# Smaller W12 loads, earlier cells and on-chip heads in the mLSTM half of a two-layer trunk

## The chip, the cores and the metric

The kernel runs on one core of a Trainium2 chip. The metric is the device time of one execution in microseconds. Three runs of the kernel before took 1699.9 to 1701.43 us, the median is 1699.91. The engines are PE (TensorE), DVE (VectorE), ACT (ScalarE), POOL (GpSimd) and SP (SyncE, which here only issues DMAs).

## The reference

The trunk has two layers on x of 512 tokens by 2048 features, all float32. Layer 0 is latent attention with 16 heads and isn't touched. Layer 1 is an mLSTM (matrix memory) with 8 heads, q and k of 128 and v of 256 features a head, and it is what the change is about:

```python
proj = x @ w_in                 # q, k, v, o, gates, z
q, k = silu(conv(q)), silu(conv(k))
# per head, equal to one causal product over the 512 tokens:
s = (q @ k.T) * DK**-0.5 * exp(decay)        # decays from the i and f gates
h = (s @ v) / max(|sum s|, exp(-m))
h = headnorm(h) * sigmoid(o) * silu(z)
x = layernorm(alpha * x + h @ w_out)
```

## The kernel before, in words

Every product is made of three passes on PE (mm3): both operands are split into a high half of a rounded type (ACT's cast, L171) and the rest (DVE's subtraction, L172). Weights come through rings in SBUF: raw (3 slots of 128x1024, 512 KB), whi and wlo (3 each) for the split halves, e (3 slots of 128x512, 256 KB), and the larger rings t, v and h. SP issues weight loads in the order that the tile framework's scheduler gives it, and each engine runs its instructions in its own order; a load that waits for a slot holds up every load behind it in SP's queue.

Layer 1 has these stages, by the time of the profile. Values by plain products end at 816 us. From 816 to 1232 five calls of quad make the other value columns and the four pairs of output gates O and Z. quad is a product of two column blocks with seven half-size products: with weight quarters W11, W12, W21, W22 (odd or even k tiles, left or right columns) its first group forms q1 (W11) and q5 (W11+W12), its second q7 (W12+W22), q6 (W11+W12+W22) and q3 (W22), its third q2 and q4. A group has four iterations, of 24, 36 and 24 matmuls; a call has 336. In the second group (L366 to L373) an iteration loads W22 and W12 as two raws, adds them in one instruction (L368), adds W22 to the kept sums t (L370), and splits all three.

From 1232 to 1430 four pairs of heads get q and k (gemm_b). The cells, one for each head, are generators that a small scheduler (tick, finish; one at a time) puts between the matmuls: a cell loads its decays (GpSimd's queue, L850), gate rows and values, makes scores (SCORES below: four blocks of 3 matmuls), exponentials (L872) and products with the values (30 matmuls), norms (L901 to L905), then yields 11 us and turns its result by 8 transposes (L907 to L912). Heads 0 to 5 store the result to a DRAM scratch gscr (L915).

From 1430 to 1697 the last projection (out_proj) multiplies the heads' results by w_out in four column blocks. The left operand comes from g1: it finishes the head's cell, reads the result back from gscr into a raw slot (L1087, k tiles 0 to 11) or takes it from SBUF (12 to 15), and splits it. Since the last cells are not done, blocks 0 and 1 are made in two parts: k tiles 0 to 11 of both, then 12 to 15 of both. Each k tile pair is one weight load (L191). The previous layer's norm gains multiply the residual on POOL (L1100, L1101); the last norm's gains and biases are broadcast by SP's queue (L1076).

Of the kernel before, what the change touches and what calls it, by code (L numbers as in the profile page):

```python
# [66 lines left out]
class Ahead:  # L67


    def __init__(self, makers, ahead):  # L70
        self.makers, self.ahead, self.items = makers, ahead, []

    def __len__(self):
        return len(self.makers)

    def __getitem__(self, i):
        while len(self.items) < min(i + 1 + self.ahead, len(self.makers)):
            self.items.append(self.makers[len(self.items)]())
        return self.items[i]


class Kern:
# [216 lines left out]
    def quad(self, w, c0, c1, x, S, done):  # L299

        nc = self.nc
        V = nc.vector
        n = KT // 2  # L310
        a, b = self.banks
        self.banks = b, a
        two = lambda f: [f(), f()]
        half = lambda v, j: v[:, 512 * j : 512 * j + 512]

        def raw(par, i, c):

            t = self.rt()
            src = w[2 * i * P : (2 * i + 4) * P, c : c + 512].rearrange("(k q p) c -> p q k c", p=P, q=2)
            nc.sync.dma_start(t.rearrange("p (k c) -> p k c", k=2), src[:, par])  # L320
            return t

        def taken(t):
            hi, lo = self.wh(), self.wl()
            self.split(t, hi, lo)
            return hi, lo

        def taken2(t):
            hi, lo = self.wh(), self.wl()
            for j in range(2):  # L330
                self.split(t[j], half(hi, j), half(lo, j))
            return hi, lo

        def mul(ps, op, j, i, hl):

            for d in range(2):
                o = op(i + d)
                for m in range(2):
                    s = slice(j * 256 + m * P, j * 256 + (m + 1) * P)
                    self.mm3(ps[m], (o[0][:, s], o[1][:, s]), (half(hl[0], d), half(hl[1], d)),  # L340
                             i + d == 0, i + d == n - 1)
                self.tick()

        xe, xo = (lambda i: x[2 * i]), (lambda i: x[2 * i + 1])
        se, so = (lambda i: S[i][0]), (lambda i: S[i][1])
        q1, q5 = two(a), two(a)
        t = []
        for i in range(0, n, 2):
            w11 = raw(0, i, c0)
            t.append([self.t(), self.t()])  # L350
            for j in range(2):
                w12 = self.e()
                kt = 2 * (i + j)
                nc.sync.dma_start(w12, w[kt * P : (kt + 1) * P, c1 : c1 + 512])
                V.tensor_tensor(t[-1][j], half(w11, j), w12, op=ALU.add)
            mul(q1, xe, 0, i, taken(w11))
            mul(q5, so, 1, i, taken2(t[-1]))
            self.some(2)
        e1, e5 = two(self.t), two(self.t)
        for m in range(2):  # L360
            nc.scalar.copy(e1[m], q1[m])
        for m in range(2):
            nc.scalar.copy(e5[m], q5[m])

        q7, q6, q3 = two(b), two(a), two(b)
        for i in range(0, n, 2):  # L366
            w22, w12 = raw(1, i, c1), raw(0, i, c1)
            V.tensor_tensor(w12, w12, w22, op=ALU.add)  # L368
            for j in range(2):
                V.tensor_tensor(t[i // 2][j], t[i // 2][j], half(w22, j), op=ALU.add)  # L370
            mul(q7, se, 1, i, taken(w12))
            mul(q6, se, 0, i, taken2(t[i // 2]))
            mul(q3, so, 0, i, taken(w22))  # L373
        u, c12 = two(self.t), two(self.t)
        for m in range(2):
            V.tensor_tensor(u[m], q6[m], e1[m], op=ALU.add)

        def sums(m):
            V.tensor_tensor(e5[m], e5[m], u[m], op=ALU.subtract)
            V.tensor_tensor(u[m], u[m], q7[m], op=ALU.add)  # L380

        def upper(m):
            V.tensor_tensor(c12[m], e5[m], q3[m], op=ALU.add)
            done(m, 1, c12[m])

        def lower(m):
            V.tensor_tensor(e5[m], e5[m], q7[m], op=ALU.subtract)
            done(2 + m, 1, e5[m])

        self.pending += [partial(f, m) for f in (sums, upper, lower) for m in range(2)]  # L390
        q2, q4 = two(a), two(a)
        for i in range(0, n, 2):
            w21 = raw(1, i, c0)
            for j in range(2):
                V.tensor_tensor(t[i // 2][j], t[i // 2][j], half(w21, j), op=ALU.add)  # L395
            mul(q2, xo, 0, i, taken(w21))
            mul(q4, xo, 1, i, taken2(t[i // 2]))
            self.some(2)

        def left(tb, v, q):  # L400
            V.tensor_tensor(v, v, q, op=ALU.add)
            done(tb, 0, v)

        self.pending += [partial(left, c + m, v[m], q[m]) for c, v, q in ((0, e1, q2), (2, u, q4)) for m in range(2)]
# [317 lines left out]

    def out_proj(self, w_out, g, resid, finish, last=1, early=0):

        nc = self.nc  # L730
        r, tasks = {}, []
        stats = {tb: self.const.tile([P, 4, 6], F32, tag="bn", bufs=4, name=self.name("bn")) for tb in range(NTB)}

        def block(toks, cb, ks=(0, KT), last=1):
            for tb in toks if ks[0] == 0 else ():
                t = r[tb, cb] = self.h() if early and cb < 2 else self.t()
                resid(tb, cb, t)
            out = self.gemm_a(w_out, cb * 512, g, toks, last, ks)
            for tb in toks:
                t = r[tb, cb]  # L740
                nc.vector.scalar_tensor_tensor(t, t, 1.0 if ks[0] else ALPHA, out[tb], op0=ALU.mult, op1=ALU.add)
                if ks[1] == KT:
                    nc.vector.bn_stats(stats[tb][:, cb], t)

        every = (0, 1, 2, 3)
        for ks in ((0, early), (early, KT)) if early else ((0, KT),):
            for cb in range(2):
                block(every, cb, ks)
        for toks in ((0, 1), (2, 3)):
            block(toks, 2)  # L750
            block(toks, 3, last=last if toks[0] else 1)
            moments = {}
            for tb in toks:
                mv, a = self.small(2, 4), self.small()
                nc.vector.bn_aggr(mv, stats[tb])
                nc.vector.tensor_scalar(a, mv[:, 1:2], EPS, None, ALU.add)
                moments[tb] = mv[:, 0:1], self.rsqrt_small(a)
            tasks.append(self.add(finish(toks, r, moments)))
        return tasks
# [90 lines left out]
            self.nc.gpsimd.dma_start(d[sb], self.R[sb][hd : hd + 1, :].broadcast_to([P, SEQ - sb * P]))  # L850
        return d

    def cell(self, hd, q, k, vscr, ascr, out, gscr, rows):


        nc, V = self.nc, self.nc.vector
# [46 lines left out]
        for tb in range(NTB):  # L903
            t = hn[tb // 2][:, tb % 2]
            nc.scalar.activation(t, t, AF.Copy, scale=y[:, tb : tb + 1])  # L905
        yield 11.0
        for j in range(2):  # L907
            tp = self.ps()
            for tb in range(NTB):
# [42 lines left out]
    def mlstm(self, w_in, x, gscr, late):  # L952
# [32 lines left out]
        for pair in range(H1 // 2):  # L985
            q_ps = self.gemm_b(w_in, 0, pair * 256, x)
            q = [self.conv_silu(q_ps[j], 2 * pair + j) for j in range(2)]
            k_ps = self.gemm_b(w_in, 0, O_K + pair * 256, x)
            k = [self.conv_silu(k_ps[j], 8 + 2 * pair + j) for j in range(2)]
            for j in range(2):  # L990
                hd = 2 * pair + j
                out = [self.h() if hd < H1 - 1 else self.e() for _ in range(2)]
                cell = self.cell(hd, q[j], k[j], vscr, ascr, out, gscr if pair < 3 else None, rows)
                t = self.add(cell, 0.0 if j else 4.0)
                tasks.append((t, out))
        return tasks

# [2 lines left out]
def hybrid_trunk_kernel(ctx: ExitStack, tc: tile.TileContext, x, positions, mla_w_in, mla_q_norm, mla_w_qb, mla_kv_norm,  # L1000
# [70 lines left out]
    K.width = 1  # L1071
    cells = K.mlstm(ml_w_in[0], x1, gscr, Turned())

    def bcast(src, cb, home=K.h):
        t = home()
        nc.sync.dma_start(t, src[0:1, cb * 512 : (cb + 1) * 512].broadcast_to([P, 512]))  # L1076
        return t

    def g1(i):
        def f():  # L1080
            task, gate = cells[i // 2]
            K.finish(task)
            hi, lo = K.h(F32R), K.h(F32R)
            t = gate[i % 2]
            if i < 12:
                t = K.rt()[:, :SEQ]
                nc.sync.dma_start(t, gscr[i * P : (i + 1) * P])  # L1087
            K.split(t, hi, lo)
            return hi, lo

        return f
# [14 lines left out]
    def finish1(toks, r, moments):  # L1106
        for tb in toks:
            for cb in range(4):
                if cb not in ln1:
                    ln1[cb] = bcast(ln_w[1:2], cb, home), bcast(ln_b[1:2], cb, home)  # L1110
                w, b = ln1[cb]
                t = r[tb, cb]
                nc.vector.scalar_tensor_tensor(t, t, moments[tb][0], w, op0=ALU.subtract, op1=ALU.mult)
# [1 line left out]
                nc.sync.dma_start(rows(out[0], tb, cb), t)  # L1115
                yield 2.0

    for t in K.out_proj(ml_w_out[0], Ahead([g1(i) for i in range(KT)], 2), resid1, finish1, 5, 12):
        K.finish(t)


# [29 lines left out]
```

## Time and profile before

| | |
|---|---|
| median of 3 runs | 1699.91 us |
| profiled execution | 1698.93 us, its span 1697.2 |
| PE busy | 1625.4 us, 96% of the span |
| DVE, ACT, POOL busy | 65%, 44%, 9% |
| DMA | 230.06 MB, 136 GB/s mean |
| mean granted TensorE clock | 0.987 |

PE is the engine that is nearly always busy, and its time is spent in one kind of instruction, a matmul of 128x512. An idle engine other than PE costs nothing by itself. What counts are the stretches in which PE's busy time is less than the stretch, or in which its granted clock is under 1.00; a wait there is followed back from PE to the engine, the load and the slot that came last.

### The profile page before, as it was taken

Reading aid. Unit: us, or ns where it says so; the run is one execution under the profiler, and the core shown is the slowest. Engines: PE = TensorE matmul, PEld = TensorE weight load, DVE = VectorE, ACT = ScalarE, POOL = GpSimd, SP = SyncE. Lnnn points to the kernel's source line nnn. Section 1 sums busy time; section 2 is a strip of 40 time slices with the busy share of each in tenths; the row PEclk is TensorE's granted clock in tenths of the full one; section 3 lists DMA queues with packets and bytes.
Section 4 is the critical chain, followed back from the end, with each engine's and each line's share of the span. In section 5 each row is a group of like instructions: output and inputs, shape, how many; then the busy total and the mean of one; then the engine's idle time right before and its main releaser. Section 6 shows DMA issues by size and latency. Waiting matters only on the chain.

```text
span 1697.2 us, 20582 instructions
## 1 busy us (share of the span) xinstructions
PE 1625.4 (96%) x7466; PEld 1338.7 (79%) x7466; DVE 1100.6 (65%) x1904; ACT 740.7 (44%) x1192; POOL 151.7 (9%) x254
## 2 busy tenths in 40 slices
PE   8999999999999999999999998998999998779996
PEld 6888888888888888778877776876788887668875
DVE  3374222677778535888686867786786566755677
ACT  3343222554555323454434544554445555553332
POOL 1000000000000000110000000000011110423600
PEclk9999999999999999999999999999999999989998
DMA  7333333322223436678555565555546842666454
GB/s 206 106 96 100 99 95 86 99 64 56 82 63 93 149 100 190 218 222 167 165 137 161 126 147 112 164 135 121 99 126 150 145 131 86 215 188 206 158 197 163
DMA packets 174182, 230.06 MB, mean 136 GB/s; under 512 B 23592, under 2 KB 97416, under 8 KB 174080
## 3 DMA queue, kind: packets, MB, share of 16 engines
q1 hardware_dynamic: 164528, 204.11, 45.2%
q0 software_dynamic: 7248, 20.44, 3.9%
q10 hardware_dynamic: 2304, 4.20, 0.8%
q8 instruction: 58, 0.95, 0.2%
q14 instruction: 44, 0.36, 0.1%
HBM read 206.51 MB, written 19.96 MB: 133 GB/s over the span
## 4 chain that ended last, share of the span: by engine, by line
PE 70%; DMA 14%; DVE 11%; issue 2%; ACT 2%; POOL 1%; SPq 0%; DVEq 0%; POOLq 0%; ACTq 0%
PE acc L206 58%; PE ps L206 10%; DMA raw<-in_ml_w_in_dram 9%; DVE wlo L172 5%; PE ps L203 2%; DMA raw<-in_ml_w_out_dram 1%; DVE raw L368 1%; ACT whi L171 1%; DMA e<-vscr 1%; DVE t L395 1%; DMA e<-in_ml_w_in_dram 1%; POOL s L264 0%; DMA gscr<-h 0%; DVE t L370 0%; DMA raw<-in_mla_w_out_dram 0%
## 5 line engine op out<-in xcount | busy, mean ns | idle before, releaser
L206 PE MATMUL acc<-whi,h 128*128 128x512 f32 x1656 | 537.8, 398 | 15.6 <-ACT whi L171 15.2
L172 DVE TENSOR_TENSOR wlo<-raw,whi 128x1024 fp32r<-128x1024 f32 (+1 forms) x311 | 377.6, 1216 | 269.0 <-ACT whi L171 254.5
L171 ACT CAST whi<-raw 128x1024 fp32r<-128x1024 f32 (+2 forms) x315 | 324.5, 1030 | 518.0 <-PE acc L206 344.7
L206 PE MATMUL acc<-h,whi 128*128 128x512 f32 x1536 | 471.9, 392 | 0.0
L206 PEld LDWEIGHTS acc<-whi,h 128*128 128x128 f32 x1656 | 315.2, 191 | 81.5 <-ACT whi L171 16.7
L206 PE MATMUL acc<-wlo,h 128*128 128x512 f32 x828 | 329.7, 398 | 12.0 <-DVE wlo L172 11.8
L206 PEld LDWEIGHTS acc<-h,whi 128*128 128x128 f32 x1536 | 286.2, 188 | 58.2 <-issue 1.0
L206 PE MATMUL acc<-h,wlo 128*128 128x512 f32 x736 | 287.4, 390 | 0.0
L206 PEld LDWEIGHTS acc<-wlo,h 128*128 128x128 f32 x828 | 158.0, 191 | 50.3 <-DVE wlo L172 18.7
L206 PEld LDWEIGHTS acc<-h,wlo 128*128 128x128 f32 x736 | 138.5, 188 | 29.5
L206 PE MATMUL ps<-whi,h 128*128 128x512 f32 x488 | 156.5, 392 | 0.0
L206 PEld LDWEIGHTS ps<-whi,h 128*128 128x128 f32 x488 | 92.4, 189 | 19.3
L206 PE MATMUL ps<-wlo,h 128*128 128x512 f32 x244 | 97.0, 397 | 10.2 <-DVE wlo L172 10.2
L171 ACT CAST whi<-t 128x512 fp32r<-128x512 f32 x120 | 68.6, 618 | 59.0 <-PE ps L206 35.3
L206 PE MATMUL acc<-whi,v 128*128 128x512 f32 x248 | 84.7, 400 | 0.0
L172 DVE TENSOR_TENSOR wlo<-t,whi 128x512 fp32r<-128x512 f32 x120 | 77.4, 685 | 9.0 <-ACT whi L171 9.0
L206 PEld LDWEIGHTS ps<-wlo,h 128*128 128x128 f32 x244 | 46.2, 189 | 23.8 <-DVE wlo L172 14.4
L203 PE MATMUL ps<-ident,t 128*128 128x128 f32 x352 | 57.6, 280 | 7.1 <-DMA t<-in_x_dram 6.4
L206 PE MATMUL ps<-h,h 128*128 128x128 f32 (+3 forms) x288 | 60.3, 323 | 4.1 <-DVE t L878 4.1
L702 ACT ACTIVATE t<-ps,s 128x128 f32<-128x128 f32 (+3 forms) x64 | 33.7, 527 | 65.2 <-DVE s L701 65.1
L203 PEld LDWEIGHTS ps<-ident,t 128*128 128x128 f32 x352 | 45.2, 144 | 20.9 <-issue 3.7
L370 DVE TENSOR_TENSOR t<-t,raw 128x512 f32<-128x512 f32 x40 | 26.6, 688 | 49.2 <-DMA raw<-in_ml_w_in_dram 49.2
(216 smaller groups left out, 1762.9 us busy)
## 6 DMA issues: line engine op xcount, KB each, us to landing
raw<-in_ml_w_in_dram SPq DMA_DIRECT2D x136, 512.0 KB, 4.9
raw<-in_mla_w_in_dram SPq DMA_DIRECT2D x48, 512.0 KB, 3.8
raw<-in_mla_w_out_dram SPq DMA_DIRECT2D x48, 512.0 KB, 3.8
raw<-in_ml_w_out_dram SPq DMA_DIRECT2D x48, 512.0 KB, 4.1
e<-in_ml_w_in_dram SPq DMA_DIRECT2D x40, 256.0 KB, 5.1
t<-in_x_dram SPq DMA_DIRECT2D x16, 256.0 KB, 6.5
raw<-in_mla_w_kvb_dram SPq DMA_DIRECT2D x16, 256.0 KB, 3.4
raw<-in_mla_w_kvb_dram SPq DMA_DIRECT2D x32, 128.0 KB, 2.6
```

The costliest lines, as they stand in the source:

```text
L171: a = self.nc.scalar.copy(hi, src)
L172: b = self.nc.vector.tensor_tensor(lo, src, hi.bitcast(F32), op=ALU.subtract)
L203: self.nc.tensor.transpose(out, in_, ident)
L206: self.nc.tensor.matmul(out, lhsT, rhs, start=start, stop=stop)
L368: V.tensor_tensor(w12, w12, w22, op=ALU.add)
L370: V.tensor_tensor(t[i // 2][j], t[i // 2][j], half(w22, j), op=ALU.add)
L395: V.tensor_tensor(t[i // 2][j], t[i // 2][j], half(w21, j), op=ALU.add)
L702: nc.scalar.activation(pt[bi], s[:, :n], AF.Exp, bias=b, scale=scale, accum_out=tot)
```

## The change

1. In quad W12 is loaded as two e tiles of 256 KB by a new helper, right(i), in the first group as before and in the second group in place of a raw; the addition and the split there are made by halves.
2. Only heads 0 to 3 go through gscr. g1 reads back k tiles 0 to 7.
3. A cell marks its task as free before the wait ahead of its transposes, and the wait is 15 in place of 11, so that the next cell can start in that time.
4. In the last projection block 0 still has k tiles 0 to 11 first, block 1 now 0 to 13; Ahead, which makes the left operands two tiles ahead, doesn't go beyond the part's last tile.
5. The last norm's broadcasts are issued by GpSimd's queue.

```diff
@@ right(i), new in quad
+            t = two(self.e)
+            for j in range(2):
+                kt = 2 * (i + j)
+                nc.sync.dma_start(t[j], w[kt * P : (kt + 1) * P, c1 : c1 + 512])
+            return t
@@ quad, second group
-            w22, w12 = raw(1, i, c1), raw(0, i, c1)
-            V.tensor_tensor(w12, w12, w22, op=ALU.add)
+            w22, w12 = raw(1, i, c1), right(i)
+            for j in range(2):
+                V.tensor_tensor(w12[j], w12[j], half(w22, j), op=ALU.add)
...
-            mul(q7, se, 1, i, taken(w12))
+            mul(q7, se, 1, i, taken2(w12))
@@ Ahead
-        while len(self.items) < min(i + 1 + self.ahead, len(self.makers)):
+        while len(self.items) < max(i + 1, min(i + 1 + self.ahead, self.limit)):
@@ out_proj
+            g.limit = ks[1]
...
-        for ks in ((0, early), (early, KT)) if early else ((0, KT),):
-            for cb in range(2):
-                block(every, cb, ks)
+        for cb in range(2):
+            block(every, cb, (0, early[cb]))
+        for cb in range(2):
+            if early[cb] < KT:
+                block(every, cb, (early[cb], KT))
@@ cell
-        yield 11.0
+
+        me[0].free = True
+        yield 15.0
@@ mlstm
-                cell = self.cell(hd, q[j], k[j], vscr, ascr, out, gscr if pair < 3 else None, rows)
+                me = []
+                cell = self.cell(hd, q[j], k[j], vscr, ascr, out, gscr if pair < 2 else None, rows, me)
                 t = self.add(cell, 0.0 if j else 4.0)
+                me.append(t)
@@ g1
-            if i < 12:
+            if i < 8:
@@ finish1
-                    ln1[cb] = bcast(ln_w[1:2], cb, home), bcast(ln_b[1:2], cb, home)
+                    ln1[cb] = bcast(ln_w[1:2], cb, home, nc.gpsimd), bcast(ln_b[1:2], cb, home, nc.gpsimd)
@@ the call
-    for t in K.out_proj(ml_w_out[0], Ahead([g1(i) for i in range(KT)], 2), resid1, finish1, 5, 12):
+    for t in K.out_proj(ml_w_out[0], Ahead([g1(i) for i in range(KT)], 2), resid1, finish1, 5, (12, 14)):
```

How this moves the queues shows at three places. SP's queue before, at the second group of the third call of quad (raw1872 and raw1873 are W22 and W12 of the first iteration; the e tiles between are the next call's):

```order
L320 DMA raw1872_8663<-in_ml_w_in_dram 128x2x512
L354 DMA e1939_9073<-in_ml_w_in_dram 128x512
L320 DMA raw1873_8665<-in_ml_w_in_dram 128x2x512
L354 DMA e1940_9076<-in_ml_w_in_dram 128x512
L354 DMA e1948_9125<-in_ml_w_in_dram 128x512
L320 DMA raw1880_8720<-in_ml_w_in_dram 128x2x512
L320 DMA raw1881_8722<-in_ml_w_in_dram 128x2x512
L320 DMA raw1888_8777<-in_ml_w_in_dram 128x2x512
L320 DMA raw1889_8779<-in_ml_w_in_dram 128x2x512
L320 DMA raw1896_8834<-in_ml_w_in_dram 128x2x512
L320 DMA raw1897_8836<-in_ml_w_in_dram 128x2x512
```

SP's queue in the same place after the change (raw1880, 1889, 1898 and 1907 are the four W22, the e tiles the halves of W12):

```order
L320 DMA raw1880_8703<-in_ml_w_in_dram 128x2x512
L328 DMA e1881_8705<-in_ml_w_in_dram 128x512
L320 DMA raw1889_8765<-in_ml_w_in_dram 128x2x512
L328 DMA e1882_8706<-in_ml_w_in_dram 128x512
L328 DMA e1890_8767<-in_ml_w_in_dram 128x512
L320 DMA raw1898_8827<-in_ml_w_in_dram 128x2x512
L328 DMA e1891_8768<-in_ml_w_in_dram 128x512
L328 DMA e1899_8829<-in_ml_w_in_dram 128x512
L320 DMA raw1907_8889<-in_ml_w_in_dram 128x2x512
L328 DMA e1900_8830<-in_ml_w_in_dram 128x512
L328 DMA e1908_8891<-in_ml_w_in_dram 128x512
```

Eight raws have become four with eight halves (e1909, the last, is the next row). The second half of an iteration (e1882, e1891, e1900) stands behind the next iteration's W22.

SP's queue before, in the last projection ahead of k tiles 8 to 11 and into block 1 (head 5's result is stored by L915 and read back by L1087 ahead of a weight tile, L191):

```order
L863 DMA t2655_12788<-ascr_6436 128x2x256
L863 DMA t2656_12789<-ascr_6436 128x2x256
L1076 DMA v2871_13918<-in_ln_w_dram 128x512
L1076 DMA v2872_13920<-in_ln_b_dram 128x512
L915 DMA gscr_83<-h2379_11589 128x512
L915 DMA gscr_83<-h2380_11590 128x512
L1087 DMA raw2648_12765<-gscr_83 128x512
L1087 DMA raw2651_12771<-gscr_83 128x512
L191 DMA raw2663_12830<-in_ml_w_out_dram 128x2x512
L191 DMA raw2720_13058<-in_ml_w_out_dram 128x2x512
L191 DMA raw2731_13112<-in_ml_w_out_dram 128x2x512
```

The same place after, from the last head that goes through gscr (head 3) on:

```order
L928 DMA gscr_83<-h2326_11268 128x512
L928 DMA gscr_83<-h2327_11269 128x512
L1102 DMA raw2591_12526<-gscr_83 128x512
L1102 DMA raw2594_12532<-gscr_83 128x512
L191 DMA raw2604_12588<-in_ml_w_out_dram 128x2x512
L191 DMA raw2632_12718<-in_ml_w_out_dram 128x2x512
L191 DMA raw2679_12918<-in_ml_w_out_dram 128x2x512
L191 DMA raw2700_13000<-in_ml_w_out_dram 128x2x512
L191 DMA raw2705_13048<-in_ml_w_out_dram 128x2x512
L191 DMA raw2717_13106<-in_ml_w_out_dram 128x2x512
L191 DMA raw2726_13173<-in_ml_w_out_dram 128x2x512
```

After head 3 weight tiles follow one another with no store, no read back and no broadcast between them.

PE before, in the fourth pair's q projection (L203 are the transposes of head 1, acc the projection; head 2's scores come 30 rows further on):

```order
L206 MATMUL acc2382_11592<-h1338_6085,whi2384_11594 128x512
L206 MATMUL acc2382_11592<-h1337_6084,wlo2385_11595 128x512
L203 MATMUL ps2386_11623<-ident_69,t2345_11394 128x128 x2
L203 MATMUL ps2386_11623<-ident_69,t2346_11395 128x128 x2
L203 MATMUL ps2387_11629<-ident_69,t2345_11394 128x128 x2
L203 MATMUL ps2387_11629<-ident_69,t2346_11395 128x128 x2
L206 MATMUL acc2381_11591<-h1344_6105,whi2400_11669 128x512
L206 MATMUL acc2381_11591<-h1345_6106,whi2400_11669 128x512
L206 MATMUL acc2381_11591<-h1344_6105,wlo2401_11670 128x512
L206 MATMUL acc2381_11591<-h1348_6120,whi2400_11669 128x512
```

PE after, in the third pair's k projection, where head 1 is turned (ps2411 is a block of head 2's scores):

```order
L206 MATMUL acc2375_11533<-h1397_6275,whi2409_11702 128x512
L206 MATMUL acc2375_11533<-h1396_6274,wlo2410_11703 128x512
L206 MATMUL ps2411_11715<-h2269_10984,h2319_11252 128x128
L206 MATMUL ps2411_11715<-h2270_10985,h2319_11252 128x128
L206 MATMUL ps2411_11715<-h2269_10984,h2320_11253 128x128
L203 MATMUL ps2412_11722<-ident_69,t2351_11406 128x128 x2
L203 MATMUL ps2412_11722<-ident_69,t2352_11407 128x128 x2
L203 MATMUL ps2413_11728<-ident_69,t2351_11406 128x128 x2
L203 MATMUL ps2413_11728<-ident_69,t2352_11407 128x128 x2
L206 MATMUL acc2375_11533<-h1403_6295,whi2409_11702 128x512
L206 MATMUL acc2375_11533<-h1404_6296,whi2409_11702 128x512
```

Head 2's scores, which stood behind head 1's transposes, now stand ahead of them, and in the projection before.

## Rows read from the trace of the kernel before

**Rows 1.** The page's part 1: busy us, share of the span, instructions.
```profile
PE 1625.4 (96%) x7466; PEld 1338.7 (79%) x7466; DVE 1100.6 (65%) x1904; ACT 740.7 (44%) x1192; POOL 151.7 (9%) x254
```

**Rows 2.** Table of stages: window, its us, busy us by engine, PEclk, DMA share, GB/s.
```profile
816.00:1232.00 416.00, 394.05 (x1683) 315.57 (x1682) 310.25 (x418) 189.37 (x260) 14.78 (x36) 0.99 0.57 135
976.00:1065.40 89.40, 80.38 (x338) 63.73 (x338) 64.14 (x87) 39.40 (x55) 2.16 (x4) 0.98 0.64 139
1065.40:1143.80 78.40, 77.58 (x337) 62.71 (x336) 63.26 (x87) 39.44 (x55) 2.16 (x4) 1.00 0.53 139
1232.00:1430.00 198.00, 198.00 (x935) 165.94 (x934) 131.64 (x227) 105.19 (x170) 22.31 (x57) 1.00 0.56 131
1430.00:1545.00 115.00, 90.64 (x427) 73.66 (x426) 73.57 (x177) 66.37 (x145) 33.92 (x55) 0.88 0.65 200
```

**Rows 3.** PE's waits, 816 to 1232: us in total, times, longest.
```profile
PE acc L206 <- DVE wlo L172: 11.1, 11, 2.4
PE ps L206 <- DVE wlo L172: 10.7, 11, 2.4
```

**Rows 4.** DVE's waits in the same stretch.
```profile
DVE t L370 <- DMA raw<-in_ml_w_in_dram: 49.2, 18, 4.4
DVE raw L368 <- DMA raw<-in_ml_w_in_dram: 26.2, 15, 3.2
DVE t L395 <- DMA raw<-in_ml_w_in_dram: 19.5, 5, 5.0
```

**Rows 5.** Chain of waits, third call of quad: start us, us, what.
```profile
1006.67 1.24 DVE raw L368
...
1010.38 6.42 DMA raw<-in_ml_w_in_dram
1016.90 1.23 DVE raw L368
...
1043.79 21.76 PE ps L206 x96
```

**Rows 6.** DVE's groups, 816 to 1232: shapes, count, busy us, mean ns, idle before.
```profile
L172 DVE TENSOR_TENSOR wlo<-raw,whi 128x1024 fp32r<-128x1024 f32 x79 | 96.0, 1221 | 2.9 <-ACT whi L171 1.2
L172 DVE TENSOR_TENSOR wlo<-t,whi 128x512 fp32r<-128x512 f32 x120 | 77.4, 685 | 9.0 <-ACT whi L171 9.0
L370 DVE TENSOR_TENSOR t<-t,raw 128x512 f32<-128x512 f32 x40 | 26.6, 688 | 49.2 <-DMA raw<-in_ml_w_in_dram 49.2
...
L368 DVE TENSOR_TENSOR raw<-raw,raw 128x1024 f32<-128x1024 f32 x20 | 24.5, 1224 | 26.2 <-DMA raw<-in_ml_w_in_dram 26.2
```

**Rows 7.** The page's part 6: count, KB, median us to landing.
```profile
raw<-in_ml_w_in_dram SPq DMA_DIRECT2D x136, 512.0 KB, 4.9
...
e<-in_ml_w_in_dram SPq DMA_DIRECT2D x40, 256.0 KB, 5.1
```

**Rows 8.** PE's waits, 1430 to 1545.
```profile
PE acc L206 <- ACT whi L171: 15.2, 5, 5.9
PE ps L206 <- DVE t L878: 4.9, 3, 3.2
```

**Rows 9.** PE's timeline there: start, us, instruction, [idle before, releaser].
```profile
1482.77 1.20 PE L206 MATMUL acc<-whi,h 128*128 128x512 f32 x4 [2.42 <-ACT whi L171]
...
1503.69 2.08 PE L206 MATMUL acc<-whi,h 128*128 128x512 f32 x4 [5.94 <-ACT whi L171]
...
1522.56 2.07 PE L206 MATMUL acc<-whi,h 128*128 128x512 f32 x4 [3.80 <-ACT whi L171]
```

**Rows 10.** SP's timeline ahead of k tiles 8 and 9.
```profile
1495.69 2.86 SPq L1087 DMA_DIRECT2D raw<-gscr  x2
1498.65 0.39 SPq L191 DMA_DIRECT2D raw<-in_ml_w_out_dram  x1
```

**Rows 11.** ACT's timeline ahead of k tiles 4 and 5.
```profile
1464.11 0.72 ACT L872 ACTIVATE t<-t,ones 128x512 f32<-128x512 f32 x1 [1.95 <-DMA t<-decay]
1464.74 1.03 ACT L171 CAST whi<-raw 128x1024 fp32r<-128x1024 f32 x1
```

More of the change, by code (lines that the diff above doesn't have):

```diff
@@ L70, in __init__ @@
     def __init__(self, makers, ahead):
-        self.makers, self.ahead, self.items = makers, ahead, []
+        self.makers, self.ahead, self.items, self.limit = makers, ahead, [], len(makers)
     def __len__(self):
@@ L321, in raw, with right @@
             return t
+        def right(i):
+            t = two(self.e)
[3 more added lines that the diff above has]
+            return t
         def taken(t):
@@ L350, in quad @@
             t.append([self.t(), self.t()])
+            w12 = right(i)
             for j in range(2):
[L352 to L355, printed above, removed]
+                V.tensor_tensor(t[-1][j], half(w11, j), w12[j], op=ALU.add)
             mul(q1, xe, 0, i, taken(w11))
@@ L721, in attend, with out_proj @@
         nc.vector.tensor_tensor(g, o, g, op=ALU.mult)
-    def out_proj(self, w_out, g, resid, finish, last=1, early=0):
+    def out_proj(self, w_out, g, resid, finish, last=1, early=(KT, KT)):
         nc = self.nc
@@ L735, in block @@
             for tb in toks if ks[0] == 0 else ():
-                t = r[tb, cb] = self.h() if early and cb < 2 else self.t()
+                t = r[tb, cb] = self.h() if cb < 2 and early[cb] < KT else self.t()
                 resid(tb, cb, t)
+            g.limit = ks[1]
             out = self.gemm_a(w_out, cb * 512, g, toks, last, ks)
@@ L851, in decays, with cell @@
         return d
-    def cell(self, hd, q, k, vscr, ascr, out, gscr, rows):
+    def cell(self, hd, q, k, vscr, ascr, out, gscr, rows, me):
         nc, V = self.nc, self.nc.vector
@@ L1072, in hybrid_trunk_kernel, with bcast @@
     cells = K.mlstm(ml_w_in[0], x1, gscr, Turned())
-    def bcast(src, cb, home=K.h):
+    def bcast(src, cb, home=K.h, eng=nc.sync):
         t = home()
-        nc.sync.dma_start(t, src[0:1, cb * 512 : (cb + 1) * 512].broadcast_to([P, 512]))
+        eng.dma_start(t, src[0:1, cb * 512 : (cb + 1) * 512].broadcast_to([P, 512]))
         return t
```

## The prediction

> **What bounds the kernel now.** I read the page's busy shares first: PE is busy for 1625.4 of 1697.2 us [rows 1], so nothing that DVE, ACT, GpSimd or a queue does can pay except where PE waits or runs at a lower clock. The table of stages says where that is [rows 2]. The four q/k projections with their cells (1232 to 1430) have PE busy for 198.00 of 198.00 us: nothing to win there, only something to lose. Two stages lose time. The five calls of quad (816 to 1232) take 416.0 us with 394.05 us of PE. The first part of the last projection (1430 to 1545) takes 115.0 us with 90.64 us of PE, at a granted clock of 0.88.
>
> For the quads the floor comes from the chain: 96 matmuls in a row take 21.76 us, or 0.2267 us each [rows 5]; a call has 336, so 76.2 us, and five have 380.8: 35.2 us are lost. The loss is uneven: the fourth call takes 78.40 us, the third, which runs the same code, 89.40 [rows 2]. What PE waits for is the low half of a split by DVE, 22 times, 21.8 us in sum [rows 3]; what DVE waits for one step earlier is a raw weight tile from HBM: 26.2 us at L368 and 49.2 us at L370, both of the second group, 19.5 us at L395, the start of the third [rows 4]. The chain of the third call shows the cycle: a load, the addition of W12 and W22 at L368, a split, and the split's end releases the slot for which the next load waited, 6.42 us in that place [rows 5]. So it is a ring that is too short for its use: an iteration of the second group takes two 512 KB raws out of three slots, lasts 36 x 0.2267 = 8.2 us when PE runs through, and the second raw of the next iteration can't be issued before W22 of this one is split. After that split come the landing (4.9 us, [rows 7]), the addition (1.22), a cast and a subtraction (1.22, [rows 6]): 7.3 us and the cast, and the split itself ends a few us into its iteration. That doesn't fit 8.2 us whenever a load is late.
>
> In the last projection PE waits 15.2 us for ACT's cast of a weight tile (5 waits) and 4.9 us for a cell's scores [rows 8]. The three large ones come straight after a cell's 30 value products: 2.42 us (k tiles 6 and 7), 5.94 (8 and 9) and 3.80 (10 and 11) [rows 9]. The casts are late because the loads are: SP's queue first waits for a head's output to be written to DRAM, then issues the loads that read it back (1495.69, 2.86 us), and only at 1498.65 the weight tile [rows 10]. With 24.4 us of idle PE and (1 - 0.88) x 115 = 13.8 us of slower clock the stage loses 38.2 us.
>
> **The change part by part.** My sums stand against the profiled execution, 1698.9 us (span 1697.2 and 1.7 around it); the median of the runs, 1699.9, is 1.0 above it, which I add at the end.
>
> W12 in halves. Per iteration of the second group one 512 KB raw goes, two 256 KB tiles of the e ring come, 20 iterations in all. Now one raw per iteration uses three slots, so W22 of the next iterations can be under way while this one is split, and the cycle above is gone. What is late next is the e ring: three slots, two tiles an iteration, each held from issue to its addition, 5.1 us of landing [rows 7] and 0.69 of addition [rows 6], at least 2 x 5.8 / 3 = 3.9 us of an 8.2 us iteration. By order the halves of the next iteration are issued between the raws, half an iteration or more ahead. So I expect every call to run like the fourth: 5 x 78.4 = 392.0, 24.0 less than 416.0 [rows 2]. I keep 2.0 of it back for the switch from the first group to the second, where raws and halves still stand in one queue: **22 us**. Bounds: 35 if all of the loss goes (416.0 - 380.8); 10 if only the waits of whole tiles go, about half of [rows 3]; below nothing only by the rival on small loads. DVE pays: 2 x 0.688 + 2 x 0.685 = 2.75 us for 1.224 + 1.221 = 2.45 [rows 6], 0.3 us an iteration, 6 us in all; DVE is busy 64.1 of 89.4 us in the third call [rows 2], so that lies in its waits; without this cover it would cost those 6 us. ACT's two casts for one are covered likewise (39.4 of 89.4). SP issues one load more, at 0.39 us [rows 10], in a queue that mostly waits for slots.
>
> The profile speaks of halves in one more way: a 256 KB tile lands in 5.1 us, a 512 KB raw in 4.9 [rows 7], so halving the size buys no latency here, and two in flight together cost none either. The Trainium skill ("DMA: Bandwidth & Descriptors", section "Bandwidth", measured) advises batching DMAs to 1 MiB or more, and its fit (section "Anatomy of one DMA") has 2.0 us of fixed cost in each; by it, as an estimate, two halves in turn need 5.2 us where one raw needs 3.2. That speaks against this edit by 2 us an iteration, 40 in all, if the loads went one after the other and were the bound: the sum would then be 1704 and not 1664.
>
> Heads 4 and 5 stay in SBUF (6 and 7 did before). Four stores and four reads of 256 KB go, and with them SP's wait for the store and the 2.86 us of reading back ahead of a weight tile [rows 10]. The waits before k tiles 8 to 11 are 5.94 + 3.80 us [rows 9]. Of the 13.8 us of slower clock, spread over five stalls, I give them two shares, 5.5 us. That is 15.2. The wait of 2.42 us stays in some form, since head 3 still takes the way through DRAM.
>
> The next cell begins before the transposes of the last one. The same matmuls in another order; one cell more (head 3) gets its scores between projection matmuls, where PE is full, and the tail has a dense cell less. That gives some of the start of the projection back, which I put at 3 us, since 38.2 less the named waits and their clock leaves about 18 us for the start, transposes and scores, of which a sixth goes. Against it: cell 5's and 7's value products now stand closer to their scores, and POOL's queue has cell 5's decay loads between L1100's multiplications, so an exponential can wait in ACT ahead of a weight cast as at 1464.11 (1.95 us for the decays, the cast behind it) [rows 11]: 3 us. The split of column block 1 at tile 14 moves two k tiles forward; it costs no instruction, and removes the wait for head 6's tiles from the end.
>
> Norm broadcasts from GpSimd: 8 issues leave SP, at 0.4 us about 3 us of a queue that held weight loads; they now stand in POOL's queue, behind cell 5's masks and ahead of cell 6's decays, and wait for v slots there. Nothing on the path either way, -2 to +2.
>
> The tail so gives 15.2 + 3 - 3 = **15 us**, between 0 (all stalls only move) and 28. In the q/k stage I take **1 us of loss** (0 to 5): the exponentials of a cell begun earlier stand in ACT ahead of weight casts.
>
> Sum: 1698.9 - 22 - 15 + 1 = 1662.9, and with the 1.0 to the median **1664 us**.
>
> **The rivals.** *Small loads are the new bound.* The e ring, not the raw ring, closes the cycle: for it speak the 5.1 us of landing and that an e load waits in SP's queue behind raws; against it 3.9 us of 8.2. Then the quads keep their 416 and only the tail moves: 1699.9 - 15 + 1 = 1686. Chance 0.12.
>
> *The tail's stalls only move.* PE stands in order, and after each cell's value products it again waits for the next weight cast, because the cell's own casts and exponentials fill ACT, not because of DRAM. For it: the waits are for ACT by name [rows 8]; against it: at 1498.65 the load itself was issued late [rows 10]. Only the quads gain: 1699.9 - 22 = 1678. Chance 0.18.
>
> *Nothing comes of it.* The raws were late through the DMA engines and not the ring (their landing of 4.9 us is a median; the share of the queues is 0.64 in the third call against 0.53 in the fourth [rows 2]), and the tail's stalls move: 1697 to 1703. Chance 0.06.
>
> *Slower.* In the stage that loses nothing today each cell is begun while the last one's work still waits; its decays aren't there, ACT stops in order at the exponential, and the weight cast behind it is late, as in [rows 11]. If each of eight cells costs a wait as long as the longest of this kind, 5.94 us [rows 9], that is 47.5 us against 36 gained: 1664 + 47.5 = 1711. It decides against the change from 4.5 us a cell on. Against it: no wait of PE in that stage now. Chance 0.05.
>
> *More than I count.* All of the quads' loss and the upper end of the tail: 1699.9 - 35 - 28 = 1637, or between that and 1646. Chance 0.03.
>
> **How the numbers follow.** The forecast's case has 0.56. Its own range is 1650 to 1676, from the bounds 10 to 35 and 0 to 28, not all at an end at once. The second rival (1678) and most of the first (1686, so to 1688) have to be inside for 8 in 10; nothing, slower and the far end stay outside: 1646 to 1688. A measurement of this kernel can't tell changes within 0.2%, 3.4 us, from none. Faster by more than that: the forecast, the first two rivals and the last, 0.89; same: 0.06, the third; slower: 0.05, the fourth.
>
> **What would show it.** Right: DVE's waits at L368 and L370 for raws fall from 75 us to under 20; the third and fifth call take 78 to 81 us; SP's queue has no store and read back for heads 4 and 5; the waits for a weight cast at k tiles 8 to 11 are under 2 us; the clock of the first part of the last projection is above 0.92. Wrong: DVE waits for e tiles in the second group (first rival); as many us of PE idle in the tail, with ACT's exponentials ahead of the casts (second); PE idle in the q/k stage (fourth).

## The result and the profile after

The changed kernel takes 1677.55 us (median of 4 runs, 1674.63 to 1680.66) where the kernel before takes 1700.67 beside it; the ratio is 0.9863, with a 95% interval of 0.984 to 0.9885. That is 23 us less; forecast were 36 (1664 us), and the range was 1646 to 1688. The profiled execution has a span of 1677.4 us.

The table of stages after (window, its us, busy us of PE, PEld, DVE, ACT, POOL, then PEclk, DMA share, GB/s) stands against [rows 2]: all five calls of quad, then the third, fourth and fifth, the q/k stage, and the start of the last projection.

```profile
816.60:1217.80 401.20, 390.56 (x1681) 316.29 (x1680) 312.36 (x458) 192.87 (x280) 14.73 (x36) 0.99 0.58 140
972.80:1057.70 84.90, 79.44 (x337) 63.76 (x336) 64.22 (x95) 40.14 (x59) 2.16 (x4) 0.98 0.67 146
1057.70:1134.40 76.70, 76.70 (x338) 63.09 (x338) 64.46 (x95) 39.90 (x59) 2.16 (x4) 1.00 0.56 145
1134.40:1217.80 83.40, 79.64 (x337) 63.83 (x336) 59.80 (x89) 39.78 (x59) 5.26 (x18) 0.98 0.58 114
1217.80:1425.20 207.40, 207.40 (x997) 174.58 (x996) 141.29 (x266) 121.51 (x205) 28.21 (x70) 1.00 0.56 138
1425.20:1503.20 78.00, 58.90 (x264) 48.13 (x264) 49.54 (x104) 42.40 (x87) 26.90 (x37) 0.85 0.62 186
```

The quads take 401.2 us, 14.8 less than 416.0. The fourth call is now near its floor (76.7 us, where 336 matmuls of 0.2267 make 76.2), but the third still takes 84.9 and the fifth 83.4. All that follows the quads took 1697.2 - 1232.0 = 465.2 us before and takes 1677.4 - 1217.8 = 459.6: 5.6 less. The q/k stage still has PE busy throughout.

PE's waits in the quads fell from 21.8 us [rows 3] to 10.6. DVE's waits after, against [rows 4]:

```profile
DVE t L402 <- DMA raw<-in_ml_w_in_dram: 38.0, 10, 5.3
DVE e L375 <- DMA e<-in_ml_w_in_dram: 21.7, 15, 4.6
DVE wlo L172 <- ACT whi L171: 18.8, 16, 7.9
DVE t L377 <- DMA raw<-in_ml_w_in_dram: 9.6, 7, 3.2
```

L375 and L377 are what L368 and L370 were: 31.3 us in place of 75.4. L402 (W21 added to the kept sum, L395 before) waits twice as long as it did (19.5 us [rows 4]).

In the last projection PE's waits after, from 1425 to 1504 (none of these four comes again later), against [rows 8]:

```profile
PE ps L206 <- ACT h L925: 7.2, 1, 7.2
PE acc L206 <- ACT whi L171: 4.5, 2, 3.9
PE ps L206 <- DVE t L889: 3.0, 1, 3.0
PE ps L206 <- DVE t L910: 1.9, 1, 1.9
```

The casts of weight tiles cost 4.5 us and not 15.2, and none of that lies ahead of k tiles 8 to 11, where [rows 9] had 9.74 (5.94 and 3.80). But there is a new wait of 7.2 us, for ACT's copy of a turned head (L925). The chain of waits behind it (start us, us, what):

```profile
1480.11 0.84 POOL v L1091 x2
1480.95 0.22 issue
1481.16 13.06 DMA t<-decay
1494.23 0.02 issue
1494.25 0.72 ACT t L883
1494.97 0.58 ACT h L925
1495.55 0.04 issue
1495.60 1.33 PE ps L206 x5
```

The head of it is one of the moved broadcasts (L1091), on GpSimd. POOL's timeline there (idle before and its releaser in brackets):

```profile
1479.51 0.60 POOL L1091 DMA_DIRECT2D v<-in_ln_w_dram  x1 [22.10 <-PE ps L206]
1480.11 0.54 POOL L1091 DMA_DIRECT2D v<-in_ln_b_dram  x1
1480.64 0.54 POOL L1091 DMA_DIRECT2D v<-in_ln_w_dram  x1
1481.16 1.06 POOL L861 DMA_DIRECT2D t<-decay  x2
```

GpSimd's queue stands for 22.1 us at a broadcast whose v slot is still in use, and head 6's decay loads (L861) are the next after the three broadcasts. They land 13.06 us after their issue, behind the broadcasts in the same queue, where the median of these loads is 4.6. ACT's exponential (L883) waits for them, and the copy that PE needs is behind the exponential:

```profile
1494.25 0.72 ACT L883 ACTIVATE t<-t,ones 128x512 f32<-128x512 f32 x1 [7.69 <-DMA t<-decay]
1494.88 1.25 ACT L925 ACTIVATE h<-ps,par 128x512 f32<-128x512 f32 x2
```

Two things come together here. ACT is free for the exponential at 1486.56 (1494.25 less 7.69), so decays issued at 1481.16 that landed in the median 4.6 us would still have been in time: the 22.1 us of standing used up all the slack that they had. Then they landed 8.5 us later than the median, while the DMA engines were busy for 95% of 1481.2 to 1494.2, at 258 GB/s. How much of that is the broadcasts ahead of them in the queue and how much SP's loads of that stretch isn't separated.

So the theory to test: the quad edit and the edits of the cells work, each for less than forecast; the moved broadcasts give some 7 us back; and what is left in quads three and five is loads. Ratios below are to the kernel before, measured beside each; intervals are 95%.

### The profile page after: what moved, and what is told of

It reads as the page before. It is cut to its first block, busy times and chain, and to the rows that moved or that the text cites. A ratio compares the mean times of both kernels' runs of the same rounds, so it can differ in the third digit from the quotient of the medians.

```text
span 1677.4 us, 20661 instructions
## 1 busy us (share of the span) xinstructions
PE 1619.5 (97%) x7466; PEld 1338.1 (80%) x7466; DVE 1108.0 (66%) x1944; ACT 748.6 (45%) x1216; POOL 158.1 (9%) x262
## 4 chain that ended last, share of the span: by engine, by line
PE 70%; DMA 12%; DVE 11%; issue 3%; ACT 2%; POOL 1%; SPq 0%; DVEq 0%; POOLq 0%; ACTq 0%
PE acc L206 56%; PE ps L206 12%; DVE wlo L172 4%; DMA raw<-in_ml_w_in_dram 4%; DMA e<-in_ml_w_in_dram 3%; PE ps L203 2%; DMA t<-decay 1%; ACT whi L171 1%; DMA raw<-in_ml_w_out_dram 1%; DMA e<-vscr 1%; DVE t L402 1%; DVE e L375 1%; POOL s L264 1%; DVE t L377 0%; DVE bn L752 0%
## 5 line engine op out<-in xcount | busy, mean ns | idle before, releaser
L172 DVE TENSOR_TENSOR wlo<-raw,whi 128x1024 fp32r<-128x1024 f32 (+1 forms) x291 | 357.7, 1232 | 260.9 <-ACT whi L171 251.1
L171 ACT CAST whi<-raw 128x1024 fp32r<-128x1024 f32 (+2 forms) x295 | 303.4, 1029 | 436.0 <-PE acc L206 323.7
L203 PE MATMUL ps<-ident,t 128*128 128x128 f32 x352 | 58.1, 282 | 9.7 <-DMA t<-in_x_dram 6.4
L203 PEld LDWEIGHTS ps<-ident,t 128*128 128x128 f32 x352 | 44.8, 144 | 23.7 <-ACT t L916 4.8
L206 PEld LDWEIGHTS ps<-h,h 128*128 128x128 f32 x288 | 48.5, 191 | 13.3 <-ACT h L925 7.5
```

Of the source, the lines that this page charges most:

```text
L171: a = self.nc.scalar.copy(hi, src)
L172: b = self.nc.vector.tensor_tensor(lo, src, hi.bitcast(F32), op=ALU.subtract)
L203: self.nc.tensor.transpose(out, in_, ident)
L206: self.nc.tensor.matmul(out, lhsT, rhs, start=start, stop=stop)
```

## The experiments

**The quad edit alone.** The kernel before with right(i) in both groups, as in the change.

> The kernel before with the edit of quad alone (W12 in 256 KB halves in both groups). In the changed kernel the five calls took 401.2 us from first matmul to the next stage's first, against 416.0 before. Theory: the raw ring's cycle is gone and nothing outside quad depends on it, so 1700.7 - 14.8 = 1686 us (1683 to 1689). Rival, as the prediction had it: 22 us from this edit, so 1679, with the rest of the gain in the changed kernel eaten by a loss elsewhere in it that the sum of stages hides.

Measured: 1682.24 us, ratio 0.9898 (0.9881 to 0.9914), 17 us less. The calls take 400.8 us in its trace, as in the changed kernel. The median lies 0.8 us below the theory's range, and by the interval (1679.5 to 1685.2 us) the rival's 1679 is only just out. A trace is one execution: in the five traces of kernels without this edit the calls take 415.9 to 419.2 us, in the five with it and no other edit of quad's code 399.0 to 402.9, and the means are 17 us apart, as the runs say. That it is the slots of the raw ring that count, and not the size or the order of the loads, rests on the waits (DVE's for raws at the two additions fell from 75.4 to 8.6 us in this trace, 7.0 and 1.6); no run gives the ring a fourth slot and keeps the whole loads.

**All but the quad edit.**

```diff
-            w22, w12 = raw(1, i, c1), right(i)
-            for j in range(2):
-                V.tensor_tensor(w12[j], w12[j], half(w22, j), op=ALU.add)
+            w22, w12 = raw(1, i, c1), raw(0, i, c1)
+            V.tensor_tensor(w12, w12, w22, op=ALU.add)
```

> The changed kernel with the edit of quad undone (one raw for W12 in the second group); all else as changed. Theory: the tail's edits are worth 5 to 8 us by themselves, so 1692 to 1696 us. Rival: the tail's edits are worth the predicted 14 and the profiled execution shows less by chance: 1687.

Measured: 1690.31 us, 0.9943 (0.9929 to 0.9957): 9.7 us by the ratio, between the two expectations. The calls take 416.1 us again, and the stall behind ACT's copy of the turned head (L918 in this kernel) is there too, at 5.1 us.

**The broadcasts back on SP, and the broadcasts on GpSimd behind the last decays.**

```diff
-  bcast(ln_w[1:2], cb, home, nc.gpsimd), bcast(ln_b[1:2], cb, home, nc.gpsimd)
+  bcast(ln_w[1:2], cb, home), bcast(ln_b[1:2], cb, home)
```

> The changed kernel with the last norm's broadcasts issued by SP again. Theory: in the changed kernel GpSimd's queue stands for 22 us at a broadcast that waits for a v slot, head 6's decay loads are behind it, ACT waits 7.7 us for them and PE 7.3 us behind ACT; with the broadcasts gone from that queue the stall goes, 7 to 10 us with the slower clock after it: 1667 to 1671 us, unless SP's queue now stands at the same slots ahead of weight tiles (then a new PE wait for a weight cast, 2 to 8 us, appears at the column blocks after k tiles 10 and 11). Rival: the decays are late for another reason (their own t slots, DRAM traffic): no change, 1677.

```diff
-        eng.dma_start(t, src[0:1, cb * 512 : (cb + 1) * 512].broadcast_to([P, 512]))
+        i = eng.dma_start(t, src[0:1, cb * 512 : (cb + 1) * 512].broadcast_to([P, 512]))
+        if eng is nc.gpsimd:
+            K.behind([i], [K.last_decay])
```

> The changed kernel with the broadcasts still on GpSimd, but ordered behind the decay loads of the last head. Theory: head 6's decays are issued some 20 us earlier, the exponential isn't waited for, PE's 7.3 us stall goes and with it some of the slower clock: 1667 to 1670 us; no wait of SP's is added, so it is at least as good as the version with SP. Rival: the stall only moves, since the same slots or ACT's order hold up the next head: 1675 to 1678.

Measured: 1670.79 us, 0.9831 (0.9814 to 0.9848), and 1670.22, 0.9826 (0.981 to 0.9843). Both are about 7 us under the changed kernel's median, as the theory said (5 to 6 by the ratios, whose intervals just meet; the slowest of their runs, 1673.0, is still under the fastest of the changed kernel, 1674.63), and neither has a PE wait for L925. In the second version GpSimd issues the first of head 6's decay loads, which the exponential needs, with no broadcast ahead of it, 24 us earlier than in the changed kernel, counted from the end of the quads (1214.8 here, 1217.8 there), and the exponential starts without a wait:

```profile
1454.49 0.60 POOL L861 DMA_DIRECT2D t<-decay  x1
...
1483.82 0.71 ACT L883 ACTIVATE t<-t,ones 128x512 f32<-128x512 f32 x1
1484.43 1.24 ACT L925 ACTIVATE h<-ps,par 128x512 f32<-128x512 f32 x2
```

**The broadcasts alone.** The kernel before with only the two calls of bcast moved to GpSimd.

> The kernel before with one edit: the last norm's broadcasts issued by GpSimd. Taking them out of GpSimd's queue made the changed kernel 7 us quicker. Theory: the price is not of the broadcasts but of their place, ahead of a head's decay loads at a time when that head's exponential is next; in the kernel before each head's scores come later, the decays have time, so the edit alone costs nothing or gives SP's 3 us back: 1697 to 1701. Rival: the edit costs its 7 us wherever it stands, by GpSimd's queue being blocked for the v slots: 1704 to 1709.

Measured: 1706.86 us, 1.0038 (1.0025 to 1.0051): slower by 6.5 us by the ratio, and its trace is 5.9 us longer behind the quads (471.1 for 465.2). My theory's number fell and the rival's holds: the edit costs its price in the kernel before too. What fell is that the decays have time there. That the place is what costs still stands, against the rival's "wherever it stands": behind the last decays, on the same queue, the broadcasts cost no more than on SP (1670.22 and 1670.79). The trace has the same picture one head later: head 7's decays behind four broadcasts that waited for a slot, an exponential that waits 4.12 us for them, and PE behind it.

```profile
1525.63 0.60 POOL L1076 DMA_DIRECT2D v<-in_ln_w_dram  x1 [12.35 <-PE ps L206]
...
1527.82 2.12 POOL L850 DMA_DIRECT2D t<-decay  x4
```

```profile
1537.35 0.72 ACT L872 ACTIVATE t<-t,ones 128x512 f32<-128x512 f32 x1 [4.12 <-DMA t<-decay]
```

```profile
1541.15 0.69 PE L203 MATMUL ps<-ident,t 128*128 128x128 f32 x2 [6.30 <-ACT t L905]
```

**Heads 4 and 5 in SBUF alone.**

```diff
-            if i < 12:
+            if i < 8:
-  gscr if pair < 3 else None
+  gscr if pair < 2 else None
```

> The kernel before with one edit: heads 4 and 5 stay in SBUF. Theory: the waits of 5.94 and 3.80 us ahead of k tiles 8 to 11 go with the slower clock behind them, as the prediction had it, 10 to 15 us: 1685 to 1690. Rival: PE waits there for ACT's own work of the cell (exponentials, casts) and not for the load, so the stalls stay: 1697 or more.

Measured: 1692.88 us, 0.9942 (0.9926 to 0.9958), 10 us; the median is 3 us outside the theory's range, and the interval (1689.2 to 1694.6 us) just reaches that range and not the rival. After its quads the trace is 8.5 us shorter than before (456.7 us for 465.2).

**The earlier cells alone.** The kernel before with the free mark and the wait of 15.

> The kernel before with one edit: a cell is marked free ahead of its transposes and the wait is 15, so that the next begins earlier. Theory: one dense cell less stands in the last projection, worth about the 3 us of the prediction or a little more: 1694 to 1698. Rival: the cells begun earlier hold ACT up in the q/k stage, which loses nothing now: 1702 to 1712.

Measured: 1694.9 us, 0.9954 (0.994 to 0.9968), 8 us by the ratio and 8.1 in the trace, more than the forecast's 3; the rival is out. ACT waits 5.15 us for late decays here as well, head 5's, with no broadcast on GpSimd's queue, and PE 3.85 us behind the cast that follows; the changed kernel has the same wait (4.63 and 3.87 us, the larger of its two waits for weight casts). The two cell edits together (with the broadcasts put right, 1666.8 - 1214.8 = 452.0 us after the quads, 13.2 less than before) are worth a little less than the sum of each alone (8.5 + 8.1 = 16.6). The 13.2 hold the split of column block 1 and the limit of Ahead too, which no run takes alone.

**Gate pairs in the order 0, 2, 1, 3.**

```diff
-        for pair in range(H1 // 2):
+        for pair in (0, 2, 1, 3):
             z = {}
```

> The changed kernel with the four gate pairs made in the order 0, 2, 1, 3. In the changed kernel the third and fifth call of quad (pairs 1 and 3) take 85.0 and 83.4 us, the second and fourth (pairs 0 and 2) 78.3 and 76.7; a 512 KB raw lands in 5.6 and 5.8 us (median) in the slow calls, 4.4 and 4.3 in the quick ones. Theory: the columns of w_in that a call reads make the transfer slower, so the slow call moves with its pair: third call (pair 2) 77 to 79 us with 4.3 to 4.6 us of landing, fourth (pair 1) 83 to 86 with 5.5 or more; time 1675 to 1680. Rival: the place of the call (which PSUM banks it starts in, what is left over from the call before) makes it slow: third 84 to 86, fourth 76 to 78.

Measured: 1674.43 us, 0.984 (0.9824 to 0.9856). The slow call moved with its pair. The third and fourth call in its trace:

```profile
971.90:1048.50 76.60, 76.60 (x337) 63.06 (x336) 64.10 (x95) 39.79 (x59) 2.17 (x4) 1.00 0.56 144
1048.50:1132.00 83.50, 78.25 (x337) 62.63 (x337) 64.05 (x95) 40.32 (x59) 2.17 (x4) 1.00 0.69 138
```

The raw's median landing is 4.8 us in the third (a little over what was expected) and 5.5 in the fourth. The DMA share is higher in the slow call at no more GB/s: the same bytes keep the DMA engines busy longer when they come from the columns of pair 1 (and 3, whose call stays the fifth and takes 83.5 us). Why these columns are slower the runs don't show.

**No loads of W12 in the second group.**

```diff
-            w22, w12 = raw(1, i, c1), right(i)
+            w22, w12 = raw(1, i, c1), two(self.e)
-                V.tensor_tensor(w12[j], w12[j], half(w22, j), op=ALU.add)
+                V.tensor_tensor(w12[j], t[i // 2][j], half(w22, j), op=ALU.add)
```

> The changed kernel without the loads of W12 in the second group of quad (the e tiles are written by the addition of the kept sum and W22 instead, so that DVE does the same work; the second group's q7 is then of other data). 20 x 512 KB of loads go. Theory: what is left of the quads' loss in the changed kernel (401.2 us of which 380.8 are matmuls) is loads that come late in the second group and at its ends, so calls three and five fall by 3 us or more each and the time to 1668 to 1672. Rival: it is the order of DVE's work, with an addition for the third group (W21) in front of splits that PE needs; W21's raw still waits for the same slots, so the calls stay at 84 and 82 and the time over 1675.

Measured: 1657.2 us, 0.9737 (0.972 to 0.9754), 20 us under the changed kernel, twice the most that the theory gave and far from the rival; 18 of them are in the calls (383.3 us for 401.2). Each of the five calls is at the floor, the third:

```profile
969.00:1045.60 76.60, 76.60 (x337) 63.02 (x337) 64.56 (x95) 39.79 (x58) 2.17 (x4) 1.00 0.56 131
```

DVE does the same work as before in it. So what is left of the quads' loss comes with the loads of W12: DVE still waits for W21 at L402, but 17.2 us and not 38.0, and PE waits nowhere in the calls. Whether these loads cost by their slots, by their places in SP's queue or by the DMA engines' time (a share of 0.56 here, 0.67 with them) this run doesn't separate.

**Additions behind the last split of the group before, halves by GpSimd's queue, and both,** on the version with the broadcasts behind the decays.

```diff
+                    self.behind([s], [cut])     # W22 from the second iteration on, and W21
```

> The version with broadcasts behind the last decays (1670.2 us), and in quad the additions of W22 (from the second iteration on) and of W21 to the kept sums are ordered on DVE behind the last split of the group before. Without the loads of W12 the five calls took 76.7 us each, so late loads are the cause of what is left. Theory: a late load costs PE only because DVE, in order, stands at an addition for the group after, ahead of a split that PE needs; with the additions behind, calls three and five fall from 84 us to 79 to 81 and the time to 1662 to 1666. Rival: the raw that the split itself needs is as late, so nothing or less than 2 us comes: 1668 to 1672.

```diff
-                nc.sync.dma_start(t[j], w[kt * P : (kt + 1) * P, c1 : c1 + 512])
+                nc.gpsimd.dma_start(t[j], w[kt * P : (kt + 1) * P, c1 : c1 + 512])
```

> The version with broadcasts behind the last decays (1670.2 us), with the 256 KB halves of W12 issued by GpSimd's queue, the raws still by SP's. Theory: a half that waits for its e slot holds up the raw behind it in SP's queue and the other way round; in two queues each goes as its own slot comes free, calls three and five fall by 3 us or more each: 1661 to 1666. Rival: the transfers and the slots are the bound and not the queue's order, or GpSimd's queue stands at the stores of the gates: 1669 to 1676.

> The two edits together (additions behind the split of the group before, halves by GpSimd's queue). Theory: each takes away a part of what a late load costs, so 1657 to 1663, near the 1650 that the version without W12's loads would have with the broadcasts behind. Rival: they take away the same stalls, so it is as good as the better one alone, within 2 us.

Measured: 1666.41 us, 0.9802 (0.9778 to 0.9826); 1689.07, 0.9928 (0.991 to 0.9946); 1681.32, 0.9885 (0.9863 to 0.9906). The first has the lowest time of all versions that compute everything, but its interval touches that of the version it starts from, and its calls take 398.9 us as there (399.0), the third still 84.0: the theory on DVE's order isn't borne out by the trace, and whether the 4 us are real is open. DVE no longer waits for W21 there, but 44.5 us for halves (36.2 and 8.3) where the version it starts from has 24.9 (24.2 and 0.7). The second is 19 us slower by the medians and 17 by the ratios, at 419.8 us for the calls, and its third call shows what it costs:

```profile
979.70:1068.20 88.50, 80.25 (x337) 63.70 (x336) 64.70 (x95) 40.18 (x58) 11.05 (x21) 0.98 0.62 133
```

The halves land in 4.4 us (median) there, and in 4.6 in the version it starts from, so the transfers aren't slower. DVE waits 41.0 us for halves (24.4 at L375 and 16.6 at L361) and not 24.9. GpSimd stands 257.2 us (141.3 and 115.9) at halves whose e slot is still in use, and 30.3 (16.2 and 14.1) at stores of values and gates that wait for DVE; which of these delays the halves that come late wasn't separated. With both edits together the calls take 412.2 us and DVE waits 70.1 us for halves (52.4 and 17.7), so this one misses its expectation in the same way.

## Why the prediction was right, and by how much each step was off

The time is inside the range that was given (1646 to 1688), but 1.6 us outside the forecast's own (1650 to 1676), and it falls on the number of the second rival, 1678, in which only the quads gain. That rival isn't what happened: PE's waits for weight casts fell from 15.2 to 4.5 us, and each cell edit gains alone. The agreement with 1678 is chance: the quads gave 5 us less than forecast, the broadcasts cost 5 to 7, and without the broadcasts' price the tail came near its sum (13.2 us less after the quads, for 15 - 1). So the range held by the room that it left for a rival, which is luck as far as the sum goes.

Three of the five signs of being right came: DVE's waits for raws at the two additions fell to 11.1 us (9.6 and 1.5), heads 4 and 5 have no store and no read back, and no weight cast is waited for at k tiles 8 to 11. Two didn't, the third and fifth call and the clock. One sign of being wrong came with them, that of the first rival: DVE waits 21.7 us for e tiles in the second group.

*The ring of raws* (22 us forecast): right in kind. The edit alone gives 17 us, its trace 15. The step that was too large is "every call to run like the fourth": I took the unevenness of the calls as the chance of a late load within a ring that is too short. It is in good part the columns that a call reads; with this edit, all loads issued by SP and the pairs in order, calls three and five stay at 82 to 86 us in every version, and the slow call moves with its pair. The sign was in [rows 2]: a DMA share of 0.64 against 0.53 at the same 139 GB/s, which I used only for the rival in which nothing comes. The first rival (the e ring as the bound) may have a part in it: DVE waits for e tiles, and without the halves' loads in the second group the calls reach 76.6 us. The 3.9 us of 8.2 that spoke against it took 5.1 us of landing for every half; in calls three and five the halves land in 6.0 and 6.5 us (median).

*Small loads.* The edit gains 17 us, so here the rows, by which a 256 KB tile and a 512 KB raw land in about the same time (5.1 and 4.9 us), were the better guide; in the edit's own trace the 256 KB tiles land in 4.7. By the Trainium skill's fit ("DMA: Bandwidth & Descriptors", section "Anatomy of one DMA") the estimate was a loss of 40 us and a sum of 1704; the section states that fit for DMAs that GpSimd issues, and these are SP's.

*Heads 4 and 5 in SBUF* (15.2 us): 10 us alone. The waits ahead of k tiles 8 to 11 went as said; the rest is that with the loads in time PE meets other waits for the same cell's work (4.8 us for L905, 0.7 before).

*Earlier cells* (3 less 3 us): 8 us alone. The price came as forecast: 3.85 us of PE behind an exponential that waits for cell 5's decays. The gain was sized too small, at 3 where the 8.1 and the price make some 12. Where it comes from shows when the q/k stage is taken to the last matmul of its projections (1432.8 before, and not the 1430 of [rows 2]) and the last projection from there to the end. Before, then with this edit alone:

```profile
1232.00:1432.80 200.80, 200.80 (x947) 168.25 (x946) 133.22 (x230) 105.97 (x171) 22.31 (x57) 1.00 0.55 129
1432.80:1697.20 264.40, 224.16 (x1027) 183.21 (x1025) 173.74 (x332) 111.70 (x200) 74.04 (x81) 0.93 0.58 185
```

```profile
1232.60:1440.00 207.40, 207.40 (x998) 174.57 (x997) 141.32 (x266) 121.46 (x205) 28.33 (x70) 1.00 0.57 138
1440.00:1689.70 249.70, 215.30 (x977) 175.96 (x975) 166.34 (x296) 100.90 (x170) 70.08 (x68) 0.94 0.57 185
```

A cell's work moves from the last projection, where PE has gaps and a granted clock of 0.93, into a stage that PE fills at 1.00: the one gets 14.7 us shorter, the other 6.6 us longer.

*The q/k stage* (1 us of loss): none, PE is busy for 207.40 of 207.40 us. The stage is longer because it holds more work (997 of PE's instructions and not 947).

*The norm broadcasts* ("Nothing on the path either way, -2 to +2"): the step that failed. I had read from the order that they stand behind cell 5's masks and ahead of cell 6's decays and wait for v slots, and priced the issue time and not what stands behind them. It costs 5 to 7 us three times over: taken out in two ways, and put alone into the kernel before. With it put right the time is 1670.2, 6 us from the forecast, of which the quads make 5.

*The clock* of the first part of the last projection, forecast above 0.92, is 0.85 over 78.0 us. That stretch holds 264 of PE's instructions and the 115.0 us before held 427, so the two don't compare; over 1425.2 to 1540.0, which holds 445, the granted clock is 0.90, still under 0.92. Over the whole last projection it is 0.93 before, 0.94 after and 0.96 with the broadcasts behind the decays, and PE is idle there for 40.2, 38.0 and 32.8 us.

## What to carry to other kernels

When a DMA moves to another engine's queue, ask first what stands behind it there and when its destination comes free: a load that nobody reads for 140 us (the broadcasts, issued at 1479.5 and first read at 1619.7) can still hold up one that is needed now. Keep a queue's next urgent load ahead of all that wait for a slot. And when the same code runs at different speed from call to call, change the order of the data before changing the code: it tells whether the place or the address is slow.

## What the runs showed of the hardware

A 512 KB tile from the same matrix, in the same pattern of rows, lands in 4.2 to 4.8 us (median of a call) from the columns of pairs 0 and 2 and in 5.4 to 5.8 from those of pairs 1 and 3, in the changed kernel and with the pairs in another order; in the changed kernel's third and fourth call the DMA engines' share is 0.67 for 146 GB/s against 0.56 for 145. And the same 256 KB halves, issued by GpSimd and not by SP, landed no later (4.4 us for 4.6) but cost the kernel 17 to 19 us.
